# Wider value products, joint runs of query and key products, and a new order of both within the heads of a hybrid decoder layer

## The chip, the cores and the metric

The kernel runs on one core of a Trainium2 chip. The metric is the device time of one execution in microseconds (us). Before the change the median of three runs is 1054.86 us (1054.76 to 1055.9).

## The reference

One decoder layer on 256 tokens with a model width of 2048, all in float32, in one launch. An input norm feeds one large projection, which is cut into a query latent and a key/value latent (512 wide each), a rotary key part (64), a gate path z (2048), four inputs of a short convolution (2048 each) and two merge gates (2048 each). Of the parts the change touches:

```
q  = rmsnorm(q_a)  @ w_q_b    -> 16 heads x (128 plain + 64 rotary)
kv = rmsnorm(c_kv) @ w_kv_b   -> 16 heads x (128 key + 128 value)
p    = softmax(causal((q_nope . k_nope + rope(q_rope) . rope(k_rope)) * scale))
attn = (p @ v) * silu(z)
u    = c_gate * c_in
conv = sum over 3 taps of conv_w[k] * shifted(u)
y_conv = (b_gate * conv * silu(z_conv)) @ w_o_conv
```

The two branches are projected, merged by sigmoid gates, projected once more, normed and added to the input.

## The kernel before, in words

Every float32 operand of a product is split into a high and a low part in TensorE's float32r type: `split_act` (L223) copies the high part on ScalarE (L224) and subtracts on VectorE for the low part (L225). A product is then three matmuls (`product`, L207: high by high, high by low, low by high), or, where both parts of one operand lie side by side in memory, one 512-column matmul with the high weight and one 256-column matmul with the low weight (`halves`, L214). `halves` does all wide ones of its list first and then all narrow ones.

Weights come as units of 128 x 2048 float32, at most. The list `plan` (L103 to L131) holds them in order of use. `load_raw` (L137) puts the DMA of a unit on SyncE's queue into one of three `raw` buffers. `split_unit` (L149) splits it in halves of 1024 columns into five `whi` and five `wlo` buffers. `take` (L192) asks for a unit when its products come, and the unit after it is split by then. So a half can be split when the half five places earlier has been used up by TensorE.

TensorE's order is fixed by the program (`keep_in_program_order`). On ScalarE and VectorE a scheduler orders most instructions by a timeline of its own, so their order is a result, not written out. PSUM results of 128 x 512 sit in tags: four banks `mm` (gate path, narrow products), two banks `cv` (channels), one `st` (scores and transposes), one `o` (attention output).

The heads' stage is the loop `for h in range(H)` (L684). Each of the 16 heads does, on TensorE:

- `project` of the gate path z: one unit, 16 matmuls of 512 columns and 16 of 256;
- `scores(h)` (L537) in the `st` bank, with a softmax on VectorE and ScalarE;
- four units of the convolution's inputs, `channels(h, 0..3)` (L619), 48 wide matmuls for two of them; head h works on block h//4 of 512 channels and on one of the four inputs, h % 4;
- `turn(h)` (L578), which transposes the softmax result after `channels(h, 1)`, and `values(h)` (L587) after `channels(h, 2)`;
- `values_next(h)` (L609), the narrow products of the next group of two heads. After the first head of a group it is `group_a` (L511): queries `qn` and keys `kn`, one unit of 2048 columns, each of the four results as 4 wide and 4 narrow matmuls. After the second it is `group_b` (L520): the rotary query `qr` and the values `vv` from one unit of 1536 columns. The values are two results of 128 tokens by 256 columns, 12 matmuls of 256 columns each.

A result in PSUM from `halves` is folded by `whole` (L343: a ScalarE copy of one half, L346, and a VectorE addition, L347) before it is split. Head 0 is special: it makes group 0 in full, does the scores late, then `group_a(1)` and `turn(0)`; `values(0)` comes in head 1.

`taps(j, t)` (L648) does the convolution's shift for one of the two token tiles: DMAs on GpSimd's queue at its start, then VectorE multiplications in the next head in two steps. For tile 1 it starts at the end of heads 1, 5, 9, 13, for tile 0 at the end of heads 2, 6, 10, 14. The product with the gate (L646) ends the fourth head of a block.

After the heads come the merge gates and the projections (`sq`, L86 by way of `tokens`) and the output (`out`); the change leaves both as they are.

Of the kernel before, what the change touches and what calls it, by code (L numbers as in the profile page):

```python
# [28 lines left out]
KR = R // P  # L29
HG = 2  # L30
NG = H // HG
EPS = 1e-6
SCALE = 1.0 / math.sqrt(DN + DR)
MASKED = -3e38
# [43 lines left out]


@with_exitstack  # L80
def tile_layer(ctx: ExitStack, tc: tile.TileContext, xw, x, pos, pvec, post_g, wc, wz, wcv, wkr, wqk, wrv, cwr, wsq, out):
    nc = tc.nc

    def matmul(*a, **kw):
# [19 lines left out]
    def add(ap, width=UNIT):  # L104
        plan.append((ap, width))
        return len(plan) - 1
# [2 lines left out]
    u_qa = [add(xw[i], 2 * XW) for i in range(KD // 2)]  # L109
    u_ckv = [add(wc[k]) for k in range(4)]  # L110
    u_kr = add(wkr, HALF)
    u_head, u_grp = [[0] * 5 for _ in range(H)], [[0, 0] for _ in range(NG)]
    order = []
    for h in range(H):
        g, second = divmod(h, HG)
        if h == 0:
            order += [(h, 0), (h, 1), (0, "a"), (0, "b"), (h, 2), (h, 3), (h, 4), (1, "a")]
        else:
            order += [(h, i) for i in range(5)]
            if g + 1 < NG:  # L120
                order.insert(-1, (g + 1, "ab"[second]))
    for i, j in order:
        if j == "a":
            u_grp[i][0] = add(wqk[i])
        elif j == "b":
            u_grp[i][1] = add(wrv[i], 3 * HALF // 2)
        else:

            u_head[i][j] = add(wcv[i, j - 1] if j else wz[i])
# [75 lines left out]
    def bank(name, tag="mm", bufs=4):  # L205
        return psum.tile([P, 512], F32, name=name, tag=tag, bufs=bufs)
# [291 lines left out]

    groups = {}

    def narrow(name, w, j, src):
        ps = bank(name)
        halves([(ps, w(j * KR + k, P), src[:, k, :], k == 0, k == KR - 1) for k in range(KR)])
        f = temp("f")
        whole(f[:, :], ps)
        return f

    def into(dst, n, f):
        split_act(dst[0][:, n, :], dst[1][:, n, :], f[:, :])

    def group_a(g):  # L511
        qn, kn = pair("qn", (P, HG, S), 2), temp("kn", (P, 2, HG, S), F32R)
        w = take(u_grp[g][0])
        for j in range(HG):
            into(qn, j, narrow(f"qn{g}_{j}", w, j, qa))
        for j in range(HG):
            into((kn[:, 0], kn[:, 1]), j, narrow(f"kn{g}_{j}", w, HG + j, ckv))
        groups[g] = [qn, kn]

    def group_b(g):  # L520
        qr, vv = temp("qr", (P, HG, S), F32R, 1), pair("vv", (P, NT, HG * DV))
        w = take(u_grp[g][1])
        f = narrow(f"qr{g}", w, 0, qa)
        rope(f[:, :], f[:, :])
        for j in range(HG):

            own, other = (slice(DR * i, DR * i + DR) for i in (j, 1 - j))
            split_act(qr[own, j, :], qr[other, j, :], f[own, :])
        for t in range(NT):
            ps = bank(f"vv{g}_{t}")  # L530
            for k in range(KR):
                c = [ckv[:, k, o + t * P : o + (t + 1) * P] for o in (0, S)]
                product(ps[:, :S], c, w(2 + k, HG * DV), k == 0, k == KR - 1)
            split_act(vv[0][:, t, :], vv[1][:, t, :], ps[:, :S])
        groups[g] += [qr, vv]

    def scores(h):  # L537

        qn, kn, qr, _ = groups[h // HG]
# [12 lines left out]
        if h == 0:  # L552
            temp("pad", (P, 4 * LINE), bufs=1)
        p = temp("p", (P, 3 * P), bufs=1)
        half = temp("sc_half", (P, P), bufs=1)
        nc.scalar.activation(half[:, :], sc[:, P:S], AF.Copy)
        nc.vector.tensor_tensor(p[:, :P], sc[:, :P], half[:, :], op=ALU.add)
        nc.vector.tensor_tensor(p[:, :P], p[:, :P], mask[:, :P], op=ALU.add)
        nc.vector.tensor_tensor(p[:, P:], sc[:, S:], mask[:, P:], op=ALU.add)
        mx, sm, rs = temp("mx", (P, NT)), temp("sm", (P, NT)), temp("rs", (P, NT))  # L560
        nb = temp("nb", (P, NT))
        for t in range(NT):
            o = slice(t * P, (2 * t + 1) * P)
# [12 lines left out]
        return p  # L576
# [8 lines left out]
        return pt  # L585

    def values(h, pt, sz):  # L587
        vv = groups[h // HG][3]
        j = h % HG
# [19 lines left out]
    def values_next(h):  # L609

        g, second = divmod(h, HG)
        if g + 1 < NG:
            (group_b if second else group_a)(g + 1)


    cv_t = cv_f[:, :, :].rearrange("p (j t k) s -> p j t (k s)", j=4, t=NT)
# [17 lines left out]
    def channels_done(j, n):  # L634
        for t in range(NT):
            ps, r = cv_ps["now"][t], r_col[:, t : t + 1]
            w, u = cv_w[:, t, :], cv_t[:, j, t, :]
            if n == 0:
                nc.scalar.activation(u, ps[:, :], AF.Copy, scale=r)
            elif n == 2:  # L640
                nc.scalar.activation(w, ps[:, :], AF.Sigmoid, scale=r)
            if n:
                dst = u if n == 1 else w
                nc.vector.scalar_tensor_tensor(dst, ps[:, :], r, dst, op0=ALU.mult, op1=ALU.mult)
            if n == 3:
                nc.vector.tensor_tensor(u, u, w, op=ALU.mult)  # L646

    def taps(j, t):  # L648

# [31 lines left out]
        yield  # L681

    cv_w = bp.tile([P, NT, 512], F32, name="cv_w")
    for h in range(H):  # L684
        sz = silu("sz", project(u_head[h][0], f"z{h}"))
        if h == 0:
            latent_turn("qa", qa, "q_g", (("st", 1), ("o", 1)))
            def turn_keys():
                latent_turn("ckv", ckv, "kv_g", (("mm", 4), ("mm", 4)))
                next(table_parts)  # L690
        else:
            if h == 1:
                values(0, pt, sz0)
            p = scores(h)
        channels(h, 0, None if h else turn_keys)
        if h == 0:
            group_a(0)
            group_b(0)
            key_rope()
        channels(h, 1)  # L700
        if h > 0:
            pt = turn(h, p)
        if h % 4 > 1:
            next(tap)
        channels(h, 2)
        if h > 0:
            values(h, pt, sz)
            if h % 4 > 1:
                next(tap)
            values_next(h)  # L710
        else:
            p = scores(h)
        channels(h, 3)
        if h % 4 in (1, 2):

            tap = taps(h // 4, 2 - h % 4)
            next(tap)
        if h == 0:
            values_next(h)
            pt, sz0 = turn(h, p), sz  # L720


    bstack.close()
# [233 lines left out]
```

## Time and profile before

| | |
|---|---|
| median of three runs | 1054.86 us |
| the profiled execution | 1054.46 us |
| its span, first to last instruction | 1052.5 us |
| granted TensorE clock, mean | 0.999 of full speed |
| heads' stage, from the first z matmul to the first `sq` matmul | 52.9 to 602.0 us |
| HBM read | 205.05 MB, 197 GB/s over the span |
| q1, all transfers of SyncE | 52.5% of 16 DMA engines |
| `raw<-wqk`, 1024 KB, issue to landing | 5.6 us (median of 8) |
| `raw<-wrv`, 768 KB, issue to landing | 4.6 us (median of 8) |

Matmuls overlap in the profile: a 512-column matmul is shown with some 0.39 us and a 256-column one with 0.28 us, but in a full row the next one starts earlier. What a matmul costs is the step from its start to the start of the next, which the timeline gives. All matmuls are recorded with one line (L86), so they are told apart by the tiles they write.

### The profile page before, as it was taken

The page shows a single profiled execution, that of the slowest core. Times are in us where ns is not written, and L with a number is a line of the kernel's source. Part 1 is how long each engine was busy: PE and PEld are TensorE (multiplying, and loading weights), DVE is VectorE, ACT ScalarE, POOL GpSimd, SP SyncE. Part 2 cuts the span into 40 slices and gives each one's busy share as a digit, 9 for nine tenths or more (in the row PEclk, how much of TensorE's full clock was granted, in tenths as well). Part 3 has the DMA queues.
Part 4 walks back from the last instruction along what each step waited for, and adds up shares of the span by engine and source line. Part 5 has one row for each costly group of instructions (what it writes and reads, how often), then busy time and mean ns, then how long its engine had stood idle before and what let it go on. Part 6 is the DMA issues. An engine that isn't in the chain of part 4 may idle for free.

```text
span 1052.5 us, 13082 instructions
## 1 busy us (share of the span) xinstructions
PE 1043.5 (99%) x5030; PEld 879.1 (84%) x5030; DVE 669.8 (64%) x962; ACT 562.9 (53%) x778; POOL 72.2 (7%) x147
## 2 busy tenths in 40 slices
PE   9999999999999999999999999999999999999997
PEld 8888888888888888888888888888888888888885
DVE  7588677865778657777676765554554455445562
ACT  6776556565665656646656464444444434443450
POOL 7610011000110001100011000000000000000000
PEclk9999999999999999999999999999999999999999
DMA  8745476554675545745466555455555555558542
GB/s 339 303 169 190 163 247 205 204 191 160 230 240 177 199 182 203 240 170 200 171 213 228 206 193 189 172 200 194 186 185 194 200 196 188 180 197 312 190 178 80
DMA packets 33310, 212.16 MB, mean 202 GB/s; under 512 B 4256, under 2 KB 4960, under 8 KB 10848
## 3 DMA queue, kind: packets, MB, share of 16 engines
q1 hardware_dynamic: 29232, 197.54, 52.5%
q0 software_dynamic: 3584, 10.50, 3.6%
q10 hardware_dynamic: 432, 3.29, 0.8%
q8 instruction: 39, 0.64, 0.2%
q14 instruction: 23, 0.19, 0.1%
HBM read 205.05 MB, written 2.10 MB: 197 GB/s over the span
## 4 chain that ended last, share of the span: by engine, by line
PE 97%; DVE 1%; issue 1%; ACT 0%; POOL 0%; POOLq 0%; DVEq 0%; ACTq 0%
PE sq L86 33%; PE cv L86 32%; PE z L86 8%; PE out L86 7%; PE kn L86 2%; PE qn L86 2%; PE qa L86 2%; PE ckv L86 2%; PE vv L86 2%; PE sc L86 1%; PE qr L86 1%; PE o L86 1%; PE tp L89 0%; PE idle L86 0%; PE kr L86 0%
## 5 line engine op out<-in xcount | busy, mean ns | idle before, releaser
L225 DVE TENSOR_TENSOR wlo<-raw,whi 128x1024 fp32r<-128x1024 f32 (+1 forms) x370 | 440.7, 1199 | 305.3 <-ACT whi L224 276.0
L224 ACT ACTIVATE whi<-raw 128x1024 fp32r<-128x1024 f32 (+1 forms) x372 | 383.8, 1036 | 366.7 <-PE sq L86 187.5
L86 PE MATMUL cv<-whi,x_both 128*128 128x512 f32 x1024 | 325.5, 391 | 0.0
L86 PEld LDWEIGHTS cv<-whi,x_both 128*128 128x128 f32 x1024 | 192.3, 188 | 38.8
L86 PE MATMUL cv<-wlo,x_both 128*128 128x512 f32 x512 | 199.6, 390 | 0.0
L86 PE MATMUL sq<-whi,x_both 128*128 128x512 f32 x512 | 160.2, 391 | 0.0
L86 PEld LDWEIGHTS sq<-whi,x_both 128*128 128x128 f32 x512 | 96.1, 188 | 19.8
L86 PEld LDWEIGHTS cv<-wlo,x_both 128*128 128x128 f32 x512 | 96.2, 188 | 18.4
L86 PE MATMUL sq<-wlo,x_both 128*128 128x512 f32 x256 | 99.6, 389 | 0.0
L86 PE MATMUL sq<-whi,at_both 128*128 128x512 f32 x256 | 80.4, 391 | 0.0
L86 PE MATMUL sq<-whi,cv_both 128*128 128x512 f32 x256 | 79.5, 389 | 0.0
L86 PE MATMUL out<-whi,m_both 128*128 128x512 f32 x256 | 79.2, 390 | 0.0
L86 PE MATMUL z<-x_both,whi 128*128 128x512 f32 x256 | 60.8, 390 | 0.0
L86 PEld LDWEIGHTS sq<-whi,cv_both 128*128 128x128 f32 x256 | 48.0, 188 | 10.0
L86 PEld LDWEIGHTS sq<-whi,at_both 128*128 128x128 f32 x256 | 48.1, 188 | 9.9
L86 PEld LDWEIGHTS out<-whi,m_both 128*128 128x128 f32 x256 | 48.0, 188 | 9.9
L86 PEld LDWEIGHTS sq<-wlo,x_both 128*128 128x128 f32 x256 | 48.1, 188 | 9.8
L86 PEld LDWEIGHTS z<-x_both,whi 128*128 128x128 f32 x256 | 47.9, 188 | 9.9
L86 PE MATMUL sq<-wlo,at_both 128*128 128x512 f32 x128 | 49.8, 389 | 0.0
L86 PE MATMUL sq<-wlo,cv_both 128*128 128x512 f32 x128 | 49.8, 389 | 0.0
L86 PE MATMUL out<-wlo,m_both 128*128 128x512 f32 x128 | 49.8, 389 | 0.0
L654 POOL DMA_DIRECT2D mv<-cv_f x24 | 12.9, 540 | 323.0 <-issue 159.7
(208 smaller groups left out, 1087.6 us busy)
## 6 DMA issues: line engine op xcount, KB each, us to landing
raw<-wsq_dram SPq DMA_DIRECT2D x80, 1024.0 KB, 4.7
raw<-wcv_dram SPq DMA_DIRECT2D x64, 1024.0 KB, 4.7
raw<-wz_dram SPq DMA_DIRECT2D x16, 1024.0 KB, 4.7
raw<-wqk_dram SPq DMA_DIRECT2D x8, 1024.0 KB, 5.6
raw<-wrv_dram SPq DMA_DIRECT2D x8, 768.0 KB, 4.6
cw<-cwr_dram POOLq DMA_DIRECT2D x24, 256.0 KB, 5.6
raw<-wc_dram SPq DMA_DIRECT2D x4, 1024.0 KB, 10.0
cv_f<-x_dram SPq DMA_DIRECT2D x1, 2048.0 KB, 9.6
```

Of the source, the lines that this page charges most:

```text
L86: return tc.keep_in_program_order(nc.tensor.matmul(*a, **kw))
L224: a = nc.scalar.activation(hi, src, AF.Copy)
L225: b = nc.vector.tensor_tensor(lo, src, hi.bitcast(F32), op=ALU.subtract)
L654: tc.keep_in_program_order(nc.gpsimd.dma_start(out=dst, in_=src))
```

## The change

The head's groups fall into three kinds instead of two. `a` is the queries and keys of two heads, `r` the rotary query of two heads, as a unit of its own with 512 columns, and `v` the values of four heads (HV = 4), a unit of 2048 columns whose matmuls have 512 columns. `narrow` takes several results at once, so that the wide matmuls of both heads come first and then the narrow ones of both. The order within the heads is new: `r` of the next group comes after the first head of a group, `a` after the second, and `v` after every fourth. Head 1 makes `a` before its own `values`, and `turn(0)` and `values(0)` move by one place each. Buffers: `qn` has one instead of two, `kn` one instead of two, `qr` two instead of one, and `vv` holds twice the columns. The shift of tile 0 starts a head later (end of heads 3, 7, 11; for the last block still head 14), and the product with the gate follows as `channels_join` at the end of the next block's first head. The weights in DRAM are laid out to fit.

```
+HV = 4
+NV = H // HV
...
+    made = {h: [] for h in range(H)}
+    for h in range(H):
+        g, second = divmod(h, HG)
+        if g + 1 < NG:
+            made[h].append(("a" if second else "r", g + 1))
+        if h % HV == HV - 1 and h + 1 < H:
+            made[h].append(("v", h // HV + 1))
+    first = [("a", 0), ("r", 0), ("v", 0)]
     order = []
     for h in range(H):
...
+        order += [(h, 0), (h, 1)] + (first if h == 0 else []) + [(h, 2), (h, 3)] + made[h] + [(h, 4)]
     for i, j in order:
...
+        if i in ("a", "r", "v"):
+            u_grp[i, j] = add({"a": wqk, "r": wqr, "v": wv}[i][j], R if i == "r" else UNIT)
...
-    def narrow(name, w, j, src):
-        ps = bank(name)
-        halves([(ps, w(j * KR + k, P), src[:, k, :], k == 0, k == KR - 1) for k in range(KR)])
-        f = temp("f")
-        whole(f[:, :], ps)
-        return f
+    def narrow(names, w, j, src):
+        pss = [bank(n) for n in names]
+        halves([
+            (ps, w((j + i) * KR + k, P), src[:, k, :], k == 0, k == KR - 1)
+            for i, ps in enumerate(pss) for k in range(KR)
+        ])
+        for ps in pss:
+            f = temp("f")
+            whole(f[:, :], ps)
+            yield f
...
     def group_a(g):
-        qn, kn = pair("qn", (P, HG, S), 2), temp("kn", (P, 2, HG, S), F32R)
-        w = take(u_grp[g][0])
...
+        qn, kn = pair("qn", (P, HG, S)), temp("kn", (P, 2, HG, S), F32R, 1)
+        w = take(u_grp["a", g])
+        for n, src, hi, lo in (("qn", qa, qn[0], qn[1]), ("kn", ckv, kn[:, 0], kn[:, 1])):
+            for j, f in enumerate(narrow([f"{n}{g}_{j}" for j in range(HG)], w, HG * (n == "kn"), src)):
+                split_act(hi[:, j, :], lo[:, j, :], f[:, :])
...
+    def group_v(v):
+
+        vv = pair("vv", (P, NT, HV * DV))
+        w = take(u_grp["v", v])
+        for t in range(NT):
+            ps = bank(f"vv{v}_{t}")
             for k in range(KR):
                 c = [ckv[:, k, o + t * P : o + (t + 1) * P] for o in (0, S)]
-                product(ps[:, :S], c, w(2 + k, HG * DV), k == 0, k == KR - 1)
-            split_act(vv[0][:, t, :], vv[1][:, t, :], ps[:, :S])
+                product(ps[:, :], c, w(k, HV * DV), k == 0, k == KR - 1)
+            split_act(vv[0][:, t, :], vv[1][:, t, :], ps[:, :])
...
+    def channels_join(j, t):
+        u, w = cv_t[:, j, t, :], cv_w[:, t, :]
+        nc.vector.tensor_tensor(u, u, w, op=ALU.mult)
...
+            channels(h, 0, turn_keys)
+            for i in first:
+                make(*i)
+            key_rope()
+            channels(h, 1)
+            channels(h, 2)
             p = scores(h)
+        elif h == 1:
+            pt = turn(0, p)
+            channels(h, 0)
+            values(0, pt, sz)
+            p = scores(h)
+            channels(h, 1)
+            channels(h, 2)
             pt = turn(h, p)
         else:
             p = scores(h)
+            channels(h, 0)
+            channels(h, 1)
+            pt = turn(h, p)
+            if tapped:
+                next(tap)
+            channels(h, 2)
+            values(h, pt, sz_new)
+            if tapped:
+                next(tap)
+        for i in made[h]:
+            make(*i)
+        if h == 1:
+            values(h, pt, sz_new)
+        sz = sz_new
         channels(h, 3)
+        if h % 4 == 0 and h > 0:
+            for t in range(NT):
+                channels_join(h // 4 - 1, t)
+        if h % 4 == 1:
+            tap = taps(h // 4, 1)
             next(tap)
+        elif h % 4 == 3 and h + 1 < H or h == H - 2:
+            tap = taps(h // 4, 0)
+            next(tap)
+    for t in range(NT):
+        channels_join(3, t)
```

`group_r`, not shown, is the first half of the old `group_b` without its values; `tapped` is true for h % 4 == 2, for h = 4, 8, 12 and for the last head.

More of the change, by code (lines that the diff above doesn't have):

```diff
@@ L80, in tile_layer @@
 @with_exitstack
-def tile_layer(ctx: ExitStack, tc: tile.TileContext, xw, x, pos, pvec, post_g, wc, wz, wcv, wkr, wqk, wrv, cwr, wsq, out):
+def tile_layer(ctx: ExitStack, tc: tile.TileContext, xw, x, pos, pvec, post_g, wc, wz, wcv, wkr, wqk, wqr, wv, cwr, wsq, out):
     nc = tc.nc
@@ L111, in tile_layer @@
     u_kr = add(wkr, HALF)
-    u_head, u_grp = [[0] * 5 for _ in range(H)], [[0, 0] for _ in range(NG)]
+    u_head, u_grp = [[0] * 5 for _ in range(H)], {}
+    made = {h: [] for h in range(H)}
[6 more added lines that the diff above has]
+    first = [("a", 0), ("r", 0), ("v", 0)]
     order = []
     for h in range(H):
[L115 to L121, printed above, removed]
+        order += [(h, 0), (h, 1)] + (first if h == 0 else []) + [(h, 2), (h, 3)] + made[h] + [(h, 4)]
     for i, j in order:
[L123 to L126, printed above, removed]
+        if i in ("a", "r", "v"):
+            u_grp[i, j] = add({"a": wqk, "r": wqr, "v": wv}[i][j], R if i == "r" else UNIT)
         else:
@@ L499, in tile_layer, with group_r @@
     groups = {}
-    def narrow(name, w, j, src):
-        ps = bank(name)
-        halves([(ps, w(j * KR + k, P), src[:, k, :], k == 0, k == KR - 1) for k in range(KR)])
-        f = temp("f")
-        whole(f[:, :], ps)
-        return f
-    def into(dst, n, f):
-        split_act(dst[0][:, n, :], dst[1][:, n, :], f[:, :])
-    def group_a(g):
-        qn, kn = pair("qn", (P, HG, S), 2), temp("kn", (P, 2, HG, S), F32R)
-        w = take(u_grp[g][0])
[L514 to L523, printed above, removed]
+    def narrow(names, w, j, src):
[8 more added lines that the diff above has]
+            yield f
+    def group_a(g):
+        qn, kn = pair("qn", (P, HG, S)), temp("kn", (P, 2, HG, S), F32R, 1)
[3 more added lines that the diff above has]
+                split_act(hi[:, j, :], lo[:, j, :], f[:, :])
+        groups["a", g] = qn, kn
+    def group_r(g):
+        qr = temp("qr", (P, HG, S), F32R)
+        (f,) = narrow([f"qr{g}"], take(u_grp["r", g]), 0, qa)
         rope(f[:, :], f[:, :])
@@ L528, in group_b, with make @@
             split_act(qr[own, j, :], qr[other, j, :], f[own, :])
+        groups["r", g] = qr
+    def group_v(v):
+        vv = pair("vv", (P, NT, HV * DV))
+        w = take(u_grp["v", v])
         for t in range(NT):
-            ps = bank(f"vv{g}_{t}")
+            ps = bank(f"vv{v}_{t}")
             for k in range(KR):
                 c = [ckv[:, k, o + t * P : o + (t + 1) * P] for o in (0, S)]
-                product(ps[:, :S], c, w(2 + k, HG * DV), k == 0, k == KR - 1)
-            split_act(vv[0][:, t, :], vv[1][:, t, :], ps[:, :S])
-        groups[g] += [qr, vv]
+                product(ps[:, :], c, w(k, HV * DV), k == 0, k == KR - 1)
+            split_act(vv[0][:, t, :], vv[1][:, t, :], ps[:, :])
+        groups["v", v] = vv
+    def make(i, j):
+        {"a": group_a, "r": group_r, "v": group_v}[i](j)
     def scores(h):
-        qn, kn, qr, _ = groups[h // HG]
+        (qn, kn), qr = groups["a", h // HG], groups["r", h // HG]
         j = h % HG
@@ L587, in values @@
     def values(h, pt, sz):
-        vv = groups[h // HG][3]
-        j = h % HG
+        vv = groups["v", h // HV]
+        j = h % HV
         o = bank(f"o{h}", tag="o", bufs=1)
@@ L607, in silu @@
         return s
[L609 to L613, printed above, removed]
     cv_t = cv_f[:, :, :].rearrange("p (j t k) s -> p j t (k s)", j=4, t=NT)
@@ L683, in tile_layer @@
     cv_w = bp.tile([P, NT, 512], F32, name="cv_w")
+    tap = None
     for h in range(H):
-        sz = silu("sz", project(u_head[h][0], f"z{h}"))
+        tapped = h % 4 == 2 or (h > 0 and h % 4 == 0) or h == H - 1
+        sz_new = silu("sz", project(u_head[h][0], f"z{h}"))
         if h == 0:
@@ L690, in turn_keys @@
                 next(table_parts)
-        else:
-            if h == 1:
-                values(0, pt, sz0)
-            p = scores(h)
[L695 to L701, printed above, removed]
-            pt = turn(h, p)
[L703 to L710, printed above, removed]
+            channels(h, 0, turn_keys)
[4 more added lines that the diff above has]
+            channels(h, 2)
+            p = scores(h)
+        elif h == 1:
[5 more added lines that the diff above has]
+            channels(h, 2)
+            pt = turn(h, p)
         else:
             p = scores(h)
-        channels(h, 3)
-        if h % 4 in (1, 2):
-            tap = taps(h // 4, 2 - h % 4)
-            next(tap)
-        if h == 0:
-            values_next(h)
-            pt, sz0 = turn(h, p), sz
+            channels(h, 0)
[12 more added lines that the diff above has]
+        sz = sz_new
+        channels(h, 3)
+        if h % 4 == 0 and h > 0:
[3 more added lines that the diff above has]
+            tap = taps(h // 4, 1)
+            next(tap)
+        elif h % 4 == 3 and h + 1 < H or h == H - 2:
[3 more added lines that the diff above has]
+        channels_join(3, t)
     bstack.close()
@@ L902, in grouped @@
         return np.ascontiguousarray(w.transpose(0, 2, 1, 3)).reshape(NG, P, -1)
-    wv = np.ascontiguousarray(wkv[:, :, DN:]).reshape(KR, P, NG, HG * DV)
-    wv = np.ascontiguousarray(wv.transpose(2, 1, 0, 3)).reshape(NG, P, -1)
+    wv = np.ascontiguousarray(wkv[:, :, DN:]).reshape(KR, P, NV, HV * DV)
+    wv = np.ascontiguousarray(wv.transpose(2, 1, 0, 3)).reshape(NV, P, -1)
     wqk = np.concatenate([grouped(wq[:, :, :DN]), grouped(wkv[:, :, :DN])], axis=2)
-    wrv = np.concatenate([grouped(wq[:, :, DN:]), wv], axis=2)
     freq = (10000.0 ** (-np.arange(0, DR, 2) / DR)).astype(np.float32)
@@ L936 @@
         "wqk": np.ascontiguousarray(wqk),
-        "wrv": np.ascontiguousarray(wrv),
+        "wqr": grouped(wq[:, :, DN:]),
+        "wv": wv,
         "cwr": np.ascontiguousarray(conv_w),
```

2 lines of the change are left out of this document (removed).

## The prediction

> **What bounds the kernel.** I read the page's busy times first, then the shares of the chain that ended last, then TensorE's timeline matmul by matmul.
>
> ```profile
> PE 1043.5 (99%) x5030; PEld 879.1 (84%) x5030; DVE 669.8 (64%) x962; ACT 562.9 (53%) x778; POOL 72.2 (7%) x147
> ...
> PE 97%; DVE 1%; issue 1%; ACT 0%; POOL 0%; POOLq 0%; DVEq 0%; ACTq 0%
> ```
>
> TensorE is busy for 99% of the span and is 97% of the chain. So the time moves only by what TensorE executes and by the moments at which it waits. VectorE (64%) matters only where it makes TensorE wait. The chain in order of time (start, length, work) gives the price of the values, here group 2's:
>
> ```profile
> 193.56 2.88 PE vv L86 x24
> 196.44 5.47 PE cv L86 x24
> 201.91 5.54 PE z L86 x32
> ```
>
> 24 value matmuls of 256 columns take 2.88 us, 120 ns each. 24 channel matmuls of twice the columns take 5.47 us, 228 ns each, not 240. The timeline of TensorE shows the steps within the narrow products and within z:
>
> ```profile
> 159.95 1.09 PE L86 MATMUL kn<-ckv,whi 128*128 128x512 f32 x4
> 160.88 0.64 PE L86 MATMUL kn<-ckv,wlo 128*128 128x256 f32 x4
> 161.36 1.09 PE L86 MATMUL kn<-ckv,whi 128*128 128x512 f32 x4
> 162.29 0.63 PE L86 MATMUL kn<-ckv,wlo 128*128 128x256 f32 x4
> 162.76 0.40 PE L86 MATMUL cv<-whi,x_both 128*128 128x512 f32 x1
> ...
> 168.25 3.79 PE L86 MATMUL z<-x_both,whi 128*128 128x512 f32 x16
> 171.87 2.08 PE L86 MATMUL z<-x_both,wlo 128*128 128x256 f32 x16
> 173.78 0.28 PE L86 MATMUL sc<-kn,qn_hi 128*128 128x256 f32 x1
> ```
>
> From start to start, z's 16 wide ones take 3.62 us (226.3 ns each), its 16 narrow ones 1.91 us (119.4 ns). The 4 wide ones of `kn`, behind narrow ones, take 0.93 us (232 ns). So each change from narrow to wide costs about 0.025 us, and it shows after the values too: the 24 `cv` behind them take 5.47 us where 24 x 226.5 is 5.44.
>
> The last thing to read is where TensorE waits at all in the heads. Of steps longer than their kind usually has I found one that names another engine, in head 0's scores:
>
> ```profile
> 86.63 0.42 DVE L225 TENSOR_TENSOR kr<-at_f,kr 128x256 fp32r<-128x256 f32 x1
> 86.66 0.22 PE L86 MATMUL sc<-kn,qn_lo 128*128 128x128 f32 x1
> ...
> 87.11 0.38 PE L86 MATMUL sc<-kr,qr 128*128 128x256 f32 x1 [0.23 <-DVE kr L225]
> ```
>
> The step from 86.66 to 87.11 is 0.45 us. In head 3 the same step is 0.07 us (173.90 to 173.97). With the next step (0.22 against 0.17 us) the wait costs 0.43 us.
>
> **The change part by part.**
>
> *Values for four heads.* Removed: 8 groups x 24 matmuls of 256 columns, 8 x 2.88 = 23.04 us. Added: 4 x 24 of 512 columns; the nearest rows are z's and `cv`'s with the same three-matmul order, 226.5 ns, so 4 x 5.44 = 21.76 us. All of it lies on the path. **-1.28 us.** Were the recovering 232 ns to hold for all 96, it would be -0.77 us; that is the unfavourable end, since `cv` rows behind narrow ones fall back to 226 within six steps.
>
> By the Trainium skill, "TensorE: Matmul & The Clock Gate", section "Back-to-back issue gap", an isolated matmul costs N/2.4 + 2.5 ns. By that rule, as an estimate, 192 x 109 ns is 20.9 us and 96 x 216 ns is 20.7 us, so the part would give 0.2 us; the trace does not agree with it at 256 columns (120 ns).
>
> *Joint runs.* The same matmuls, but 8 wide and 8 narrow in a row instead of twice 4 and 4. A group then changes from narrow to wide twice instead of four times. 8 groups x 2 changes x 0.025 = 0.40 us. From this I take off 0.1 us, because a run of 8 recovers in full within itself where a run of 4 was cut short. **-0.30 us**, with 0 and -0.45 as ends.
>
> *`r` by itself.* The same 4 wide and 4 narrow matmuls. They now change to `cv` (0.03 to 0.05 us) where `vv` did before (0.03 us). **0**, at most +0.15 us. The transposes and outputs of heads 0 and 1 change neighbours only: +0.05 us at most, from a transpose that now stands before `cv` or `qn` instead of z.
>
> *The wait in head 0.* TensorE now comes 5.44 - 2.88 = 2.56 us later to these scores. What stands on VectorE ahead of `kr` grows too. In the changed program's order on VectorE: 1024 columns of weights more up to channel unit 2, then r1 (512 columns) and both halves of channel unit 3 where there was one half of `a`. In columns it is 9216 against 8704, 0.6 us at 1.14 us per 1024 (the rate back to back); two value splits of 512 columns cost 0.68 us (the `mv` rows' size) where two of 256 cost 0.34, +0.7 us. So `kr` comes 1.3 us later and TensorE 2.56 us later: the wait of 0.43 us should be gone with 0.8 us to spare. **-0.43 us**; 0 if the split of channel unit 3 is itself late.
>
> *New waits.* Two results at once take two of four `mm` banks. At the end of heads 3, 7 and 11 `vv` takes the bank of `qn`, 2.79 us after the joint `qn` run (8 x 226.5 + 8 x 120 + 0.03). Ahead of its drain on VectorE stands one weight half (1.22 us) that the run itself releases, then the addition (0.42 us): 1.7 us, so 1.1 us is left. In head 0 `qr` takes the bank of the first `qn` at 71.3 us; three weight halves now stand ahead of that addition, where 512 and 1024 columns did (2.03 us). It ended at 69.9 us; 3 x 1.14 - 1.9 = 1.5 us more make 71.4, but VectorE should start them about 0.5 us earlier, because the piece split ahead of the latent's transposes is 0.70 instead of 1.23 us. I expect 70.9 us, 0.4 us early; at most it is +0.9 us late, if nothing is gained there and one ScalarE half (1.06 us) is behind too. Behind these waits stands all of TensorE.
>
> *Everything else is hidden.* `a` is needed 11 us after it is made (`channels(h, 3)` 5.47 and z 5.54 us) and takes four drains of 1.7 us. The softmax result reaches TensorE as before:
>
> ```profile
> 153.26 0.55 DVE L225 TENSOR_TENSOR pt<-tp,pt 128x384 fp32r<-128x384 f32 x1
> ...
> 156.58 0.39 PE L86 MATMUL o<-pt,vv_hi 128*128 128x512 f32 x1
> ```
>
> It is done 2.8 us ahead, and the changed program's order keeps the same one weight half in front of it. VectorE loses 16 x 0.42 us of value splits and gains 8 x 0.69. SyncE issues 20 loads instead of 16 for the groups (0.33 us each, bytes the same, 14.3 MB); a 512-column unit holds one of three `raw` buffers, which shortens the lead by some 4 us of TensorE time against weight halves that, by the timeline, are split 5 to 10 us before their first use. Without that cover, each late unit would cost its lateness once. GpSimd's tap DMAs of tile 0 move by one head, and the multiplications that need them move with them.
>
> Sum: -1.28 - 0.30 - 0.43 + 0.05, about **-2.0 us**. On the profiled execution (1054.46 us) that is 1052.5; this lies 0.4 us below the median of the runs shown, 1054.86, so against the median it is **1052.8 us**. A measurement of this kernel can tell about 0.2% from no change, 2.1 us; the forecast lies almost on that bound.
>
> **The rivals.**
>
> *The wait returns.* `kr` stays late (0.43 us) or `qr` waits for its bank (up to 0.9 us), or `vv` does in three heads by tenths. For it: VectorE is the bound of that stretch, 4.82 and 4.90 of 5 us busy in the windows 70 to 75 and 75 to 80. Against: the sums above. Time: -1.0 to -1.6, about 1053.5 us. Chance 0.14.
>
> *The step goes with the columns.* If a 512-column value matmul cost twice 120 ns, the values would give nothing and only 0.7 us would remain: 1054.1 us. The `cv` and z rows, with the same operand sizes, speak against it. Chance 0.04. The Trainium skill's rule, named above, would leave about the same.
>
> *Slower: the softmax result is late for the values.* In heads 2 to 15 `pt` has 2.8 us to spare. If the scheduler's order, as it turns out on the chip, puts over 2.8 us more ahead of it on VectorE (three more weight halves are 3.4 us), each head loses the rest, 14 x 0.6 = 8.4 us: 1061 us. Against: that order has the same work there, and VectorE has room (26.0 of 35 us busy from 100 to 135; `v` adds 5.44 us of TensorE for 2 x 1.22 + 2 x 0.69 = 3.8 us of it). Chance 0.06.
>
> *More than forecast.* The changes between narrow and wide vanish altogether (0.45 us) and some wait that I did not see goes: 1052.3 us or less. Chance 0.09.
>
> **How the numbers follow.** The forecast keeps 0.67. Its own scatter of 0.3 us and that of the runs (0.1 us below to 1.0 us above the median) spread it evenly over the bound of 0.2%, 1052.75 us: 0.34 past it, 0.33 short of it. Faster: 0.34 + 0.09 = 0.43. Within: 0.33 + 0.14 + 0.04 = 0.51. Slower: 0.06. The range leaves out the slower case, the far end of the second rival and the tail of the fourth: 1052.1 to 1053.9 us.
>
> **What would show it.** The values' 24 matmuls in a row should take 5.44 us, 8 wide ones of the second joint run 1.84 us and 8 narrow ones 0.95 us. The scores of head 0 should show no wait for `kr`, and `qr` in head 0 and `vv` in heads 3, 7, 11 should start right behind the matmul ahead of them. The prediction is wrong if VectorE's name stands as a releaser in front of any of these, or if a head outside them is longer than before by more than its narrow products.

## The result, and the profile after

The changed kernel takes **1053.1 us** (median of 16 runs, 1052.41 to 1053.57), the kernel before in the same comparison 1054.93 us (16 runs, 1054.44 to 1055.9). The ratio is 0.9982, 95% interval 0.9975 to 0.9990: 1.83 us less, 0.17%, just inside the bound of 0.2% that I had set for a difference that can be told from none. The interval ends below 1, so the time did fall. The forecast was 1052.8 us in a range of 1052.1 to 1053.9. A second set of 11 runs of the changed kernel (`after_again`, below) gave 1053.12 us.

The profiled execution took 1052.91 us with a span of 1050.9 us, against 1054.46 and 1052.5 us before. The page of the changed kernel, busy times and shares of the chain that ended last:

```profile
PE 1041.9 (99%) x4934; PEld 874.3 (83%) x4934; DVE 670.0 (64%) x954; ACT 560.3 (53%) x770; POOL 71.4 (7%) x147
...
PE 98%; issue 1%; DVE 0%; POOL 0%; ACT 0%; POOLq 0%; DVEq 0%; ACTq 0%
```

TensorE executes 96 matmuls fewer (5030 - 4934: the values), is busy for 1.6 us less, and has risen from 97% to 98% of the chain. VectorE's 1% of the chain is gone. Before, the chain left TensorE at 74.40 us, ran through VectorE and came back at 87.11 us at the wait for `kr`; now it stays on TensorE through head 0. The share (12 us) is not the price of that wait (0.43 us): the chain follows the engine that was late, however little it was late.

The chain in order of time (start, length, work), from the keys of the third group on:

```profile
190.16 2.79 PE kn L88 x16
192.95 5.47 PE vv L88 x24
198.42 5.44 PE cv L88 x24
203.86 5.54 PE z L88 x32
```

The values of four heads are now 24 matmuls that take 5.47 us together, where two groups took 2 x 2.88 = 5.76 us. The channel products behind them take 5.44 instead of 5.47 us, since they no longer stand behind narrow matmuls; the values themselves do, and lose the same 0.03 us.

TensorE's timeline of the second joint run in head 1, and what follows it:

```profile
123.99 2.00 PE L88 MATMUL kn<-ckv,whi 128*128 128x512 f32 x8
125.83 1.12 PE L88 MATMUL kn<-ckv,wlo 128*128 128x256 f32 x8
126.78 0.40 PE L88 MATMUL o<-pt,vv_hi 128*128 128x512 f32 x1
```

From start to start, 8 wide ones take 1.84 us and 8 narrow ones 0.95 us, as the prediction asked for.

The timeline of all engines around head 0's scores:

```profile
87.65 0.42 DVE L229 TENSOR_TENSOR kr<-at_f,kr 128x256 fp32r<-128x256 f32 x1
...
89.39 0.22 PE L88 MATMUL sc<-kn,qn_lo 128*128 128x128 f32 x1
...
89.45 0.34 PE L88 MATMUL sc<-kr,qr 128*128 128x256 f32 x1
```

`kr` is done at 88.07, and its first reader starts at 89.45, 0.06 us behind the matmul ahead of it, with no releaser named. The softmax result of head 2, in the same view:

```profile
152.70 0.55 DVE L229 TENSOR_TENSOR pt<-tp,pt 128x384 fp32r<-128x384 f32 x1
...
156.01 0.39 PE L88 MATMUL o<-pt,vv_hi 128*128 128x512 f32 x1
```

It is done 2.8 us ahead, as before. Over all heads the lead is 2.4 to 2.9 us (before 2.5 to 2.8).

Because TensorE is never idle for long, the time can be accounted for step by step: I added the distances from the start of each matmul to the start of the next, by the result that the first one makes. The difference of the two profiled executions, changed minus before:

| steps of | us |
|---|---|
| `vv` (23.04 to 21.89) | -1.15 |
| `cv` | -0.18 |
| `sc` (the wait in head 0) | -0.44 |
| `kn`, `qn`, `qr` (-0.08) and `z` (-0.11) | -0.19 |
| `qa`, the first products of the program | +0.18 |
| all steps, with the small rest | -1.77 |
| from the last matmul's end to the end of the span (7.68 to 7.90) | +0.23 |
| span | -1.54 |

The line of `qa` is scatter of the start: over all profiled executions of this study, in which that stage is the same, it ranges from 22.0 to 23.4 us. The line at the end is not scatter; `six_more_loads`, below, is about it. It is read from the last matmul, in the timeline of the kernel before and then of the changed one, and from the spans (1052.49 and 1050.94 us):

```profile
1044.42 0.39 PE L86 MATMUL out<-whi,m_both 128*128 128x512 f32 x1
```

```profile
1042.65 0.39 PE L88 MATMUL out<-whi,m_both 128*128 128x512 f32 x1
```

### The profile page after: what moved, and what is told of

The parts are those of the page before. It is cut to its first block, busy times and chain, and to the rows that moved or that the text cites. A ratio compares the mean times of both kernels' runs of the same rounds, so it can differ in the third digit from the quotient of the medians.

```text
span 1050.9 us, 12889 instructions
## 1 busy us (share of the span) xinstructions
PE 1041.9 (99%) x4934; PEld 874.3 (83%) x4934; DVE 670.0 (64%) x954; ACT 560.3 (53%) x770; POOL 71.4 (7%) x147
## 4 chain that ended last, share of the span: by engine, by line
PE 98%; issue 1%; DVE 0%; POOL 0%; ACT 0%; POOLq 0%; DVEq 0%; ACTq 0%
PE cv L88 33%; PE sq L88 33%; PE z L88 8%; PE out L88 7%; PE qn L88 2%; PE kn L88 2%; PE qa L88 2%; PE vv L88 2%; PE ckv L88 2%; PE sc L88 1%; PE qr L88 1%; PE o L88 1%; PE tp L91 0%; PE idle L88 0%; PE kr L88 0%
## 5 line engine op out<-in xcount | busy, mean ns | idle before, releaser
L88 PEld LDWEIGHTS z<-x_both,wlo 128*128 128x128 f32 x256 | 32.8, 191 | 1.2
```

Source lines behind the costliest of these rows:

```text
L88: return tc.keep_in_program_order(nc.tensor.matmul(*a, **kw))
```

## The experiments

My theory was the sum of the prediction: fewer and wider value matmuls, fewer changes between wide and narrow, and one wait that went. The rivals were that the step goes with the columns, that waits move rather than go, and that something outside the change makes the difference. Each experiment takes one of these apart. Ratios are to the kernel before.

### The width of the value products

`values256` and `values128`: the changed kernel, with each result of 512 value columns made in pieces of 256 or 128 columns (the diff is that of 256).

```
+            for q in range(0, HV * DV, 256):
+                qs = slice(q, q + 256)
+                for k in range(KR):
...
+                    product(ps[:, qs], c, [x[:, qs] for x in w(k, HV * DV)], k == 0, k == KR - 1)
```

> The changed kernel, but each value result is made in two pieces of 256 columns (192 matmuls again, in the changed places, from the same units). Theory: the width is worth 120.0 ns against 226.5 to 228 ns a pair, so this gives back 23.04 - 21.89 = 1.15 us: 1054.25 us on the changed kernel's 1053.1, and 120 ns steps in the value rows. Rival (the step goes with the columns, the gain came from order and waits): no difference from the changed kernel, 1053.1 us, steps of 113 to 114 ns.

> The changed kernel, but each value result is made in four pieces of 128 columns: 384 matmuls. Theory (a matmul takes at least about 120 ns from start to start because its weight load does): 384 x 120 = 46.1 us for 21.9, 24.2 us more, 1077.3 us. Rival one (steps go with the columns, 60 ns as the single 128-column matmuls of scores and outputs show): 384 x 60 = 23.0 us, 1.2 us more, 1054.3 us. Rival two (each matmul has a fixed extra of some 7 ns over its columns, which 120 against 113 ns would also give): 384 x 64 = 24.6 us, 2.7 us more, 1055.8 us.

Measured: `values256` 1054.36 us (11 runs), ratio 0.9996 (0.9987 to 1.0005); `values128` 1074.04 us (4 runs), ratio 1.0182 (1.0168 to 1.0196). The chain of `values256`, and then that of `values128`, at the first values:

```profile
72.67 5.75 PE vv L88 x48
```

```profile
72.77 10.67 PE vv L88 x96
```

In the changed kernel the same place is 5.49 us with 24 matmuls. All value steps together are 21.89 us with 512 columns, 23.03 with 256 and 42.69 with 128: medians of 227, 120 and 111 ns per matmul. So the width is worth 1.15 us of the values' own steps and 0.10 us of `cv`'s behind them, 1.25 us in all, and the times say 1054.36 - 1053.1 = 1.26 us; the rival by which the step goes with the columns falls. Between 256 and 128 columns a matmul gets hardly shorter: in a row of 128-column matmuls, each with a 128x128 weight of its own, the step stays at about 111 ns. Against the 512 columns of the changed kernel that costs 20.8 us, where 24.2 had been expected from 120 ns; both rivals (60 and 64 ns) fall. Single 128-column matmuls in the scores do take 60 ns, so the limit is one of the row and not of a single matmul. That the weight load is its reason is not shown.

### The joint runs

`separate`: the changed kernel with the wide and narrow matmuls of each result in a run of their own.

```
-        halves([
-            (ps, w((j + i) * KR + k, P), src[:, k, :], k == 0, k == KR - 1)
-            for i, ps in enumerate(pss) for k in range(KR)
-        ])
+        for i, ps in enumerate(pss):
+            halves([(ps, w((j + i) * KR + k, P), src[:, k, :], k == 0, k == KR - 1) for k in range(KR)])
```

> The changed kernel, but queries and keys of the two heads run one after the other again (4 wide, 4 narrow, 4 wide, 4 narrow). Theory: two more changes from narrow to wide per group, 16 x 0.025 us less some 0.1: 0.2 to 0.4 us more, 1053.4 us, with 232 ns steps at the start of each 4 wide ones. Rival: the changes cost nothing of their own, the time stays at 1053.1 us. The profile decides, as the runs scatter by as much.

Measured: 1053.63 us (11 runs), ratio 0.9988 (0.9979 to 0.9997). TensorE's timeline of `separate` at the same keys as above:

```profile
125.11 1.09 PE L88 MATMUL kn<-ckv,whi 128*128 128x512 f32 x4
126.03 0.64 PE L88 MATMUL kn<-ckv,wlo 128*128 128x256 f32 x4
126.51 1.09 PE L88 MATMUL kn<-ckv,whi 128*128 128x512 f32 x4
...
127.91 0.40 PE L88 MATMUL o<-pt,vv_hi 128*128 128x512 f32 x1
```

From 125.11 to 127.91 is 2.80 us, against 2.79 in the joint run. The sums over the program are `kn` +0.13, `qn` +0.05, `cv` +0.04 and `vv` +0.04 us: the joint runs give 0.26 us. Of the times' 0.5 us some 0.3 lies in the span, where these steps and the start's scatter are (medians 1051.4 against 1051.1 us); the rest lies outside the span, 2.3 instead of 2.0 us.

`alternate` and `before_alternate` try the opposite order in both kernels: in `halves` each narrow matmul stands right behind its wide one, so every run has length 1.

```
-        for ps, w, both, first, _ in blocks:
+        for ps, w, both, first, last in blocks:
             matmul(ps[:, :], w[0], both, start=first, stop=False)
-        for ps, w, both, _, last in blocks:
             matmul(ps[:, :S], w[1], both[:, :S], start=False, stop=last)
```

> The changed kernel, but halves puts each narrow matmul right behind its wide one (wide, narrow, wide, narrow) for z, queries, keys and rotary queries. Theory (a matmul lasts its columns, 226.6 and 113.3 ns, and some 7 ns more only where its weight load comes late; two loads of at least 111 ns fit under 340 ns): z's 256 narrow ones fall from 119.4 to 113.3 (-1.6 us), the 160 others too (-1.0), and the slow wide ones behind narrow runs go (-0.7): 1049.8 us on 1053.1. Rival one (each change from narrow to wide costs 0.025 us): some 370 more changes, +9.4 us, 1062.5. Rival two (the 120 and 235 ns steps belong to the neighbours, whatever the load): 416 wide ones at 235, +2.6 us, 1055.7.

> The kernel before with the same alternation of wide and narrow matmuls and nothing else. Theory: z -1.6, the other narrow ones -1.0, the slow wide ones behind them -1.0: 1051.3 us on 1054.93. What is then left to the changed kernel with alternation is the width of the values (1.15) and the wait in head 0 (0.43), as the joint runs have nothing to give any more: a difference of 1.5 to 1.6 us. Rival (joint runs and order have a worth of their own): a difference of 1.8 us as without alternation.

Measured: `alternate` 1054.58 us (11 runs), ratio 0.9996 (0.9988 to 1.0005); `before_alternate` 1056.99 us (11 runs), ratio 1.0020 (1.0011 to 1.0029). TensorE's timeline of z in `alternate`:

```profile
163.94 0.39 PE L88 MATMUL z<-x_both,whi 128*128 128x512 f32 x1
164.17 0.28 PE L88 MATMUL z<-x_both,wlo 128*128 128x256 f32 x1
164.28 0.40 PE L88 MATMUL z<-x_both,whi 128*128 128x512 f32 x1
164.51 0.28 PE L88 MATMUL z<-x_both,wlo 128*128 128x256 f32 x1
164.63 0.40 PE L88 MATMUL z<-x_both,whi 128*128 128x512 f32 x1
```

My own theory for this pair, a gain of some 3 us from a narrow weight load beside a wide matmul, fell. A pair of z takes 352.5 ns on the mean (235.6 + 116.9), in runs 346.6 (227.0 + 119.5). A wide matmul right behind a narrow one is 8.6 ns dearer, a narrow one behind a wide one 2.6 ns cheaper; over 256 pairs that is +2.19 - 0.67 = +1.52 us. The +9.4 us of rival one was far too much. Rival two comes nearest: its 235 ns are what z's wide ones take, and its +2.6 us are too much because the narrow ones got cheaper and queries, keys and rotary queries lost nothing (-0.17 us). As to what a change in a run costs, TensorE's timeline of the other kernels tells it: the first five wide ones behind a narrow one mostly take 228 to 236 ns each, together some 0.02 to 0.03 us, about what I had read (0.04 where `cv` stood behind the keys before). In the kernel before, alternating made the wait for `kr` in head 0 longer as well (steps of `sc` +1.04 us), so that it came to 1056.99 instead of the 1051.3 us expected. The two alternating kernels are 2.41 us apart, where I had expected 1.5 to 1.6: the steps of `sc` make 1.50 us of it, those of `vv` 1.01.

`joint4` goes the other way: 16 wide and then 16 narrow matmuls for the queries and keys of two heads together, which takes all four `mm` banks at once. `joint4_v_first` is the same with `v` made ahead of `a`, and in head 0 in the order `r`, `v`, `a`.

```
+        for (hi, lo), f in zip(dst, narrow(names, w, 0, [qa, qa, ckv, ckv])):
+            split_act(hi, lo, f[:, :])
...
```

> The changed kernel with queries and keys of both heads in one run: 16 wide, then 16 narrow. Theory: one change from narrow to wide less per group (8 x 0.03 = -0.2 us), but the values in heads 3, 7 and 11, and the rotary query in head 0, take the bank of the first query result 0.95 us after the last query matmul instead of 2.8; in the changed kernel that bank is free 1.9 us after it. So TensorE waits 0.9 us in four places: +3.4 us, 1056.5 us on 1053.1, with VectorE's f named ahead of vv and qr. Rival (the banks do not bind, or the scheduler brings the drains forward): 1052.9 us.

> The same run of 16 and 16, and the values ahead of queries and keys (in head 0 rotary query, values, then queries and keys), so that no product takes a bank that was filled just before. Theory: the gain of one change per group without the waits: -0.2 us, 1052.9 us on 1053.1, the best version so far by less than the runs scatter; the profile shows it in the steps of kn's wide matmuls, 226.6 ns. Rival: the new order costs a wait elsewhere (the key's split for head 0's scores, or the scores of the next head), then VectorE is named there.

Measured: `joint4` 1057.62 us (10 runs), ratio 1.0026 (1.0017 to 1.0036); `joint4_v_first` 1058.33 us (5 runs), ratio 1.0036 (1.0024 to 1.0049). TensorE's timeline of `joint4` at the end of head 3:

```profile
192.97 1.12 PE L88 MATMUL kn<-ckv,wlo 128*128 128x256 f32 x8
194.85 0.50 PE L88 MATMUL vv<-whi,ckv 128*128 128x512 f32 x1 [0.77 <-DVE f L351]
```

The step from the last `kn` (193.81) to `vv` is 1.05 instead of 0.12 us: `vv` needs the bank of `qn`, and VectorE's addition that drains it comes late, because `qn` ends one run later. The same stands ahead of `qr` in head 0 and of `vv` in heads 7 and 11. Four times 0.93 is 3.7 us, and the first `vv` and `qr` steps behind it are 0.1 us longer each; with 0.2 us of start that is the 4.3 us that the span of the profiled execution grew (the times' 4.5 us hold some 0.3 us outside the span). The bank theory was right, at a price somewhat above the 3.4 us that I had expected.

In `joint4_v_first` the three waits before `vv` are gone, and a larger one stands in head 0:

```profile
75.06 1.07 PE L88 MATMUL kn<-ckv,whi 128*128 128x512 f32 x4
78.85 2.08 PE L88 MATMUL kn<-ckv,whi 128*128 128x512 f32 x4 [2.71 <-DVE vv_lo L229]
80.72 1.72 PE L88 MATMUL qn<-qa,wlo 128*128 128x256 f32 x8
```

The second `kn` waits for the bank of a value tile, which VectorE drains 2.9 us late, for VectorE is the bound of that stretch (4.88 of 5 us busy from 70 to 75). My expectation of 1052.9 us was wrong by that place. Behind the wait there is a second loss, read below.

`joint4_mixed` puts this right: runs of four results in all groups but the first, `v` ahead of `a`.

> Joint runs of four results for every group except the first, which keeps two runs of two; in heads 3, 7 and 11 the values now come ahead of the queries and keys. My theory (bank waits alone ate the gain of the longer runs: about 1.03 us ahead of the first group's rotary query, and three times 1.05 us ahead of the values, by the timeline of the kernel with runs of four): all four waits are gone, the 16 wide matmuls of seven groups lose one change from narrow to wide each, 7 x 0.025 = 0.2 us, and the time is 1052.9 us, which cannot be told from 1053.1 by the times but can in the trace (no wait of TensorE named after VectorE in the heads, wide key products shorter in sum by 0.15 us). Rival one, the waits come back elsewhere (the second key product waits for the bank of the second value tile in heads 3, 7, 11): a step of 0.5 to 1 us in three places, 1054.5 to 1056 us. Rival two, the long runs themselves are slower, not the waits: the time stays at 1057 us with no step over 0.3 us.

Measured: 1053.15 us (11 runs), ratio 0.9984 (0.9975 to 0.9993). No step in the heads names VectorE or is over 0.32 us, so the waits, with the loss behind the longest of them, had made the two versions before slow, and not the long runs. The wide steps of `qn` and `kn` are 0.27 us shorter, but narrow ones (+0.10), `cv` (+0.08) and `vv` (+0.05) are longer: 0.05 us are left of the expected 0.2. Runs longer than eight bring nothing here.

### The wait for `kr`

`before_early_key`: the kernel before, with the rotary key made ahead of the second half of the first group.

```
             group_a(0)
+            key_rope()
             group_b(0)
-            key_rope()
```

> The kernel before, with the rotary key made ahead of the rotary query and the values of group 0 instead of behind them. Theory: the wait of 0.43 us in head 0's scores goes, nothing else changes: 1054.5 us on 1054.93. Rival: VectorE is the bound from 68 to 87 us, so its 2.5 us of key work ahead of the drains makes the rotary query or the values wait for their banks: the wait moves, 1054.9 us or more.

Measured: 1054.93 us (11 runs), ratio 1.0001 (0.9992 to 1.0010). The scores' steps lose 0.44 us, as in the changed kernel, but the timeline of TensorE's weight loads shows it again a little earlier:

```profile
71.62 0.77 PEld L86 LDWEIGHTS qr<-qa,whi 128*128 128x128 f32 x4 [0.19 <-DVE f L347]
...
73.42 0.19 PEld L86 LDWEIGHTS vv<-whi,ckv 128*128 128x128 f32 x1 [0.34 <-DVE f L347]
```

`qr` and `vv` wait for banks that VectorE drains later now. Steps of `kn` +0.15, `qr` +0.39, `vv` +0.09 take back 0.63 us. On an engine that is the bound of its stretch an earlier place for one operation is a later one for another; the wait moves and doesn't go. In the changed kernel `kr` comes later, not earlier (88.07 against 87.05 us); what got rid of the wait there is TensorE's work ahead of these scores, 2.56 us more of it. `late_values` takes all 5.4 us of the values away from there, so that TensorE has less to do ahead of the scores than even before the change: the values of the first four heads are made behind head 0's scores.

```
-    first = [("a", 0), ("r", 0), ("v", 0)]
+    first = [("a", 0), ("r", 0)]
+    made[0].append(("v", 0))
```

> The changed kernel, but the values of heads 0 to 3 are made after head 0's scores instead of ahead of its channels. Theory: their 5.44 us of TensorE were the cover under which VectorE finishes the rotary key; without them TensorE comes to the scores at 83.8 us, and the key's split stands behind a weight half that waits until then for its buffer: 1.2 + 0.4 us of wait, 1054.7 us on 1053.1, with VectorE's kr named ahead of the scores. Rival (the wait went through VectorE's new order, not through the cover): no wait, 1053.1 us.

Measured: 1058.03 us (6 runs), ratio 1.0033 (1.0021 to 1.0045), 4.9 us above the changed kernel. The timeline of all engines:

```profile
84.18 0.22 PE L88 MATMUL sc<-kn,qn_lo 128*128 128x128 f32 x1
...
84.58 2.35 DVE L230 TENSOR_TENSOR wlo<-raw,whi 128x1024 fp32r<-128x1024 f32 x2
86.85 0.42 DVE L230 TENSOR_TENSOR kr<-at_f,kr 128x256 fp32r<-128x256 f32 x1
87.33 0.38 PE L88 MATMUL sc<-kr,qr 128*128 128x256 f32 x1 [2.93 <-DVE kr L230]
```

The wait is back, with 3.15 us for a step of 0.06, twice what I had expected, since two weight halves stand ahead of `kr` on VectorE. That explains 3.1 of the 4.9 us. The rest is in the next view, the windows of the same kernel (columns: window, its length, then busy time and instructions of PE, PEld, DVE, ACT, POOL, the granted TensorE clock, and the share and rate of the DMAs):

```profile
84.00:87.30 3.30, 0.40 (x3) 0.21 (x2) 3.24 (x5) 1.36 (x2) 0.00 (x0) 1.00 0.42 179
87.30:90.00 2.70, 2.67 (x12) 2.34 (x13) 1.34 (x5) 0.33 (x2) 0.00 (x0) 0.70 0.77 243
90.00:92.00 2.00, 2.00 (x8) 1.70 (x7) 1.14 (x2) 1.98 (x3) 0.00 (x0) 0.56 0.47 197
```

TensorE is busy throughout from 87.3 on, but from 88.4 to 91.8 its clock is halved, and the steps of `qr` and `vv` grow by 1.55 us.

### The end of the program

Every other kernel with the changed loads takes 7.90 to 7.97 us from its last matmul to its end, every one with the loads of before 7.68. The prediction had put the loads down as hidden. SyncE issues 20 loads for the groups instead of 16. At the end it waits for eight semaphores of the DMAs in a fixed order, about 0.06 us each, and the DMAs it issues take these semaphores in turn. In the program before, the last output has the sixth of them, in the changed one the second: so six waits instead of two stand behind its landing. `six_more_loads` tests it: six loads of the square weights are made in two halves each, which should move the last output to the eighth place.

```
+        if i in u_d[1][0] + u_d[2][0][:2]:
+            cuts = (0, w // 2, w)
```

> The changed kernel with six of the loads of the square weight matrices each made in two halves, so that SyncE issues six loads more. What it tests is the 0.23 us by which every kernel with the changed loads is longer than before after its last matmul (7.90 to 7.97 us against 7.68 us). My theory: at the end SyncE waits for eight semaphores of the DMAs in a fixed order, 0.06 us each; the loads take them in turn, and four more loads moved the one of the last output from the sixth to the second place, so that six waits instead of two stand behind its landing. With six more it is in the eighth place: the end after the last matmul is 7.90 - 6 x 0.061 = 7.54 us, the span 0.36 us shorter, about 1052.75 us by the times. Rival: the 0.23 us is due to something else at the end (more semaphores to clear, later landing of the last output): the end stays at 7.90 us. Second rival: the halves delay a weight of the later stages and TensorE waits: the sum of its steps grows, by 0.1 us or more for each.

Measured: 1052.64 us (10 runs), ratio 0.9978 (0.9968 to 0.9987). From the last matmul to the end it is 7.53 us, where 7.54 was expected, and the steps of TensorE are those of the changed kernel but for the start (`qa` +0.51 us). The records of SyncE's waits in the traces leave no other place for it: from the issue of the last output to the wait that sees it landed it is 2.11 us before, 2.10 in the changed kernel and 2.09 here, and from there to the last of the eight waits 0.12, 0.37 and 0.00 us. So the four loads did cost 0.23 us, by their number alone, and this version is the shortest of the study.

### The changed kernel again

> The changed kernel as it is, for comparison on the same chip: 1053.1 us by every theory, and the same steps; only the first products of the query latent, which wait for the first weights, should differ from run to run.

Measured: 1053.12 us (11 runs), ratio 0.9983 (0.9974 to 0.9992). All steps are the same within a few hundredths but for the start, `qa` +0.33 us.

## Why the prediction was right, point by point

| step of the prediction | expected, us | measured, us |
|---|---|---|
| values for four heads | -1.28 | -1.25 (`values256`: `vv` 1.15, `cv` 0.10) |
| joint runs | -0.30 | -0.26 (`separate`) |
| `r` by itself, neighbours of heads 0 and 1 | +0.05 | -0.01 (the -1.52 of `vv`, `cv`, the narrow products and z, less the two above) |
| wait in head 0 | -0.43 | -0.44 |
| new waits | 0 | 0 |
| number of loads | hidden, 0 | +0.23 |
| sum | -2.0 | -1.73; by the times -1.83 |

**Values.** The price of 226.5 ns was right as a mean of `vv` and what follows it. The 24 in a row take 5.47 instead of 5.44 us because they stand behind narrow matmuls; the `cv` behind them get it back. The Trainium skill, "TensorE: Matmul & The Clock Gate", section "Back-to-back issue gap", gives its N/2.4 + 2.5 ns for an isolated matmul; as an estimate from it, 256 columns would have been 109 ns and 0.2 us all that there was to win. `values256` measures 120 ns and 1.25 us in its stream of matmuls with a new weight each, so here the measurement decides.

**The wait.** `kr` comes 1.0 us later than before (88.07 against 87.05; 1.3 expected), and TensorE reaches its reader 1.4 us after it (0.8 expected). The sum on VectorE was 0.3 us too careful, on the safe side, and 0.2 of it is one term: it took 0.68 us for a value split of 512 columns, which is how long one is shown, and 0.34 for one of 256, which is a step. By steps it is 0.60 and 0.34, so the two splits add 0.5 us and not 0.7. As `kr` itself comes later, it is TensorE's work ahead of these scores that removes the wait and not the order on VectorE, and `late_values` shows the wait come back without that work.

**New waits.** `vv` in head 3 starts at 192.79 right behind the last `kn`, and its bank was drained at 191.91, 0.9 us before (1.1 expected); `qr` in head 0 follows at 71.51 a bank drained at 70.86, 0.65 us before (0.4 expected). Both margins are small, and `joint4` shows what stands behind them: the same two places wait as soon as `qn` ends one run later.

**The step that failed** is the one on SyncE's loads, "bytes the same", costed at nothing. Their issue is hidden indeed, but their number decides at which place of the closing waits the last output stands: 0.23 us.

**The rivals.** No wait returned, the step does not go with the columns, and the softmax result keeps its 2.4 to 2.9 us. The forecast of a gain of 2.0 us lay on the bound of 0.2%, and the 1.83 us fell inside it. The forecast of 1052.8 us lies 0.3 us below the median; 0.1 of it is rounding (1054.86 - 1.96 is 1052.9), and the closing waits, with 0.23 us, are more than what is left.

## What to carry to other kernels

Where one engine is 99% busy, price an edit by start-to-start steps of its own instructions by width, and add what stands right behind: a wide matmul behind a narrow one pays some 2 to 9 ns for a few steps, whichever result it belongs to. Ahead of every wider or longer run ask whose bank it takes and when that is drained: runs of four results cost 4.1 us through four bank waits and gained 0.05 us without them. An order that puts work between a late operand and its reader removes a wait; one that shuffles the engine which is the bound only moves it.

## What the runs showed of the hardware

**A long wait costs more than its length.** After the wait in `late_values` (a step of 3.15 us, 2.9 of them idle) TensorE's granted clock was 0.5 for 3.41 us (88.38 to 91.79), which cost another 1.55 us. In `joint4_v_first` (a step of 3.10 us, 2.7 idle) it was 0.5 from 78.64 to 82.06 us, with steps of 427 and 213 ns. The steps of 1.05 us in `joint4` show no such thing. The Trainium skill, "TensorE: Matmul & The Clock Gate", section "What's actually happening", tells of a clock gate that halves the clock after an idle window of about 3.4 us, with windows of 3413 ns that run freely. The windows are in these traces too: in the clock records of all fourteen profiled executions the changes lie whole multiples of 3.413 us apart (24, 1 and 281 in `late_values`). But a window need not be idle throughout: in `late_values` TensorE had been at work again for 1.05 us when the clock fell. From their first change on, cut into these windows, the fourteen traces show a halved clock behind each window with 2.07 us or more without a matmul, the program's end included, and behind none with 1.47 us or less. What holds between the two is not shown.

**Some 13 ns more per matmul at full clock.** At half clock the steps are 426 to 427 and 213 to 214 ns for 512 and 256 columns, in proportion to the columns. At full clock, in runs of one width, they are 226.5 and 120, 13 ns above half of these. So two matmuls of 256 columns cost about 13 ns more than one of 512, which is what the values gained; with 128 columns in a row the step is 111 ns, and another limit holds.

**The semaphore of the last output counts.** SyncE's closing waits come one after the other, about 0.06 us each, and only those behind the last landing cost time; moving that output from the second place to the eighth gave 0.37 us in the trace.
